# A layer's k/v projection by feature tiles over four odd token chunks, and its input's even halves made between the evacuations

## The chip, the cores and the metric

The kernel runs on one core of one Trainium2 chip. The core has five engines that work through queues of their own, each strictly in the order in which the program wrote its instructions: PE (TensorE, the matmuls), DVE (VectorE), ACT (ScalarE), POOL (GpSimd) and SP (SyncE, which here only issues DMAs). They wait for each other through semaphores. The metric is the device time of one execution in microseconds; the profile is one such execution, taken by the hardware profiler.

## The reference, cut to what matters

The reference is one inference step of a trunk of two layers over 1024 prompt tokens and 8 decode tokens, with a model width of 1024. Layer 1 is a retention layer, layer 2 a sliding-window attention layer with two k/v heads of 64 each. Each layer starts with an RMSNorm of its input and ends with an output projection that is added to its input.

```python
h = rmsnorm(x, g_norm)
proj = h @ w_in
q, k, v, gate = jnp.split(proj, [SWA_Q, SWA_Q + SWA_KV, SWA_Q + 2 * SWA_KV], axis=-1)
k = rmsnorm(k.reshape(B, L, SWA_KV_HEADS, SWA_HD), k_gain)
v = v.reshape(B, L, SWA_KV_HEADS, SWA_HD)
```

The change sits at the border of the two layers: at the end of layer 1's output projection, which makes x, and at the start of layer 2, which makes k and v (256 columns together) for all tokens before anything else.

## The kernel before, in words

**Numbers in two halves.** All float32 products are made of three matmuls on a rounded type: a number is split into a high part (ACT rounds it) and a low part (the number less its high part, on DVE or POOL), and high times high, high times low and low times high are added up in PSUM. Such a pair for a weight is called woh and wol in layer 1 and pw in layer 2; the pair for layer 2's input is A_hi and A_lo. It is kept in four pairs of tiles `AT[q]`, each for two tiles of 128 features and all tokens. `a_split(k, par)` makes the part of feature tile k for the even (par 0) or odd (par 1) chunks of 128 tokens, from a copy of x that `a_load` brings back from the scratch `xscr` in DRAM.

**Layer 1's output projection.** It is done in eight sets (`osets`): four groups of 256 features, in two parts that are summed. A set has seven products by a Strassen-like scheme, A11, A12, S4, S2, S1, S3 and A22, each for two halves t of the tokens; every (product, t) is a slot of 12 matmuls, so a set has 14 slots. The last set (group 3 in part 1) makes features 768 to 1023, which are feature tiles 6 and 7. S2 opens a new pair of banks `po`, S3 the next pair, and A22 adds on top of S3's banks once S3 has been read out of them. The read-outs (`o_evac`) are on ACT and DVE. Then `out_b` adds what part 0 left (`pa_add`), makes A_hi and A_lo of feature tiles 6 and 7 at once, stores x, and `out_sq` adds its squares to `acc`.

**The table.** In this stage the order of all engines but PE is written by a small planner, `Table`. `tb.slot` lists PE's slots with a clock of planned times, `tb.when(t, ...)` lists work that is written behind the slot in which time t lies, and `tb.later(n, ...)` work that is written behind slot n. `osets[7].n0` is the first slot of the last set and `e7` its planned time. Work listed behind slot n0 + 13 comes when all slots are written. `late` gives how many slots after a product `out_b` follows in the last set. The weights of the k/v projection are loaded by `kvs_load` and split by `kvs_conv`; those of the first q projection are loaded by `w0_load` into the same two raw tiles, so that SP's queue holds at these loads until a conversion has freed a tile.

**Layer 2's start.** Nine chunks of tokens (eight of the prompt, chunk 8 for the decode tokens) go through the projection in the order `KORD`: 1, 3, 5, 7, then 0, 2, 4, 6, 8. `kv_mm(c, h)` is half h of a chunk: four feature tiles of three matmuls into one bank. The loop over n writes half 0 of the next chunk, then half 1 of this one, and behind it the other steps of earlier chunks: `kv_ev` (norm of k through `knorm_a` and `knorm_b`: a square on ACT, kss on DVE, krk on POOL, kd on DVE; v on ACT and DVE), `kv_tr` (transposes of kd on PE into one of two banks `tr`) and `kv_kk` (keys out of that bank, on ACT and DVE). `rstd9` makes the norm factors r of layer 2's input from `acc`, once for the odd and once for the even chunks: small matmuls on PE, r and e on DVE, a power on POOL. `rb_dg`, `rb_mm` and `rb_ev` spread r over partitions: three scaled identity matrices (diagonals), a matmul with ones, and a copy to `rbc`. `a_dec` makes the decode columns of A, `xdec2` is the stationary tile of chunk 8's matmuls, copied from these columns. The conversions of the first weight sets (`wts[0].conv`, `wts[1].conv`) lie in the same loop, one piece per step, on ACT and POOL. Behind the loop starts `pair_proj`, the stream of q and gate projections, with q0; from there the matmuls are written by a credit scheme that the change does not touch.

Of the kernel before, what the change touches and what calls it, by code (L numbers as in the profile page):

```python
# [7 lines left out]
F32 = mybir.dt.float32  # L8
F32R = mybir.dt.float32r
AF = mybir.ActivationFunctionType  # L10
ALU = mybir.AluOpType
# [4 lines left out]
NP = 1024  # L16
ND = 8
NT = NP + ND
# [55 lines left out]
def _trunk(ctx, tc, nc, a):  # L74
# [588 lines left out]
    n = 0  # L663
# [610 lines left out]
    def a_dec():  # L1274
        nc.sync.dma_start(out=xscr[:, :, NP:NT].rearrange("f p n -> p f n"), in_=xd)
        xg = odT[:, 0:8, :]
        dve.tensor_tensor(xg, xd, gcol[:, 16:24].unsqueeze(2).broadcast_to([128, 8, ND]), MUL)
        for q in range(4):
            ahi, alo = [y[:, :, NP:NT] for y in AT[q]]
            dve.tensor_copy(ahi, xg[:, 2 * q:2 * q + 2, :])  # L1280
            dve.tensor_tensor(alo, xg[:, 2 * q:2 * q + 2, :], ahi.bitcast(F32), SUB)

    def o_slot(s, j, t):
# [16 lines left out]
        if done and t == 1:  # L1300
            late = {"A12": 6, "S1": 4, "S3": 2, "A22": 1}[name] if fin else {"S1": 5}.get(name, 2)
            tb.later(n + late, out_b if s.part else out_a, s, *done)
# [9 lines left out]
    for s in osets:  # L1312
# [28 lines left out]
        if s.part == 0:  # L1341
            tb.when(first["A22"] - 7.0, res_diff, s)
        elif s.q:
            tb.later(s.n0 + 11, pa_add, s, "p", pool)

# [124 lines left out]
    for i in range(4):  # L1470
        tb.when(e7 + 11.0 + 1.9 * i, kvs_conv, i)
    for j in range(2):
        tb.when(e7 + 13.5 + 3.5 * j, w0_load, j)
    for k in range(6):
        m = e7 + 3.1 + 2.0 * k
        tb.when(m - 5.0, a_load, k, 1)
        tb.when(m, a_split, k, 1)
    for k in range(2):
        tb.when(e7 + 11.0 + k, a_load, k, 0)
        tb.when(e7 + 15.6 + 2.0 * k, a_split, k, 0)  # L1480
    tb.ev.sort(key=lambda e: e[:2])
# [231 lines left out]

    def kv_mm(c, h):

        if h == 0:
            kvst[c] = (pjp.tile([128, 512], F32, tag="pj", name="pj") if KORD.index(c) % 4 < 2 else
                       scp.tile([128, 512], F32, tag="sc", name="sc"))
        ps = kvst[c]
        cs = slice(c * 128, c * 128 + 128)  # L1720
        for k in range(4 * h, 4 * h + 4):
            if c == 8:
# [55 lines left out]
    def rb_dg(ti):  # L1778
        t0, t1 = TG[ti]
        dg = io("sq", 2)  # L1780
        if ti == 2:
            nc.gpsimd.memset(dg[:, 256:264], 0.0)
        for i in range(3):
            c = t0 // 128 + i
            m = 128 if c < 8 else ND
            nc.vector.tensor_scalar(dg[:m, i * 128:i * 128 + m], ident[:m, :m], r9[:m, c:c + 1], None, ALU.mult)
        return dg
# [567 lines left out]

    dgs, rbs = {}, {}
    kv_mm(KORD[0], 0)
    for n in range(9):
        if n < 8:
            kv_mm(KORD[n + 1], 0)  # L2360
        if n == 1:
            rstd9(1)
        if n == 3:
            rstd9(0)
        if n >= 3:
            kv_tr(KORD[n - 3])
        kv_mm(KORD[n], 1)
        if n >= 4:
# [3 lines left out]
        if n >= 1:  # L2372
            kv_ev(KORD[n - 1])
        for k in ((), (2, 3), (4, 5))[n] if n < 3 else ():
            a_split(k, 0)
        if n == 2:
            a_dec()
# [6 lines left out]
        if 5 <= n <= 8:  # L2384
            wts[1].conv(n - 5)
        if n == 4:
            for q in range(4):
                nc.vector.tensor_copy(xdec2[:, 2 * q:2 * q + 2, 0:8], AT[q][0].bitcast(F32)[:, :, NP:NT])
                nc.vector.tensor_copy(xdec2[:, 2 * q:2 * q + 2, 32:40], AT[q][1].bitcast(F32)[:, :, NP:NT])
        for ti in list(dgs):  # L2390
# [14 lines left out]
    fill(ps, 1.5)  # L2405
    kv_kk(2)
    for ti in list(rbs):
        rb_ev(ti, rbs.pop(ti))
# [126 lines left out]
```

## Time and profile before

| | us |
|---|---|
| median of the three runs shown | 1329.73 (1326.33 to 1332.76) |
| the profiled execution | 1329.56 |
| its span, first to last instruction | 1327.7 |
| PE busy | 1275.8 (96% of the span) |
| DVE / ACT / POOL busy | 861.4 / 708.6 / 847.8 |
| last set of layer 1's output projection, first matmul | 860.5 |
| first matmul of the k/v projection | 886.5 |
| first matmul of q0 | 920.4 |

A row of the timeline has the start in us, the duration in us, the engine, the line, the operation with its output and input by their names, the shape and how many were merged; in brackets at the end stand the engine's idle time ahead of it and what ended that. Matmuls are pipelined, so the duration of one (0.28) is longer than the distance to the next (0.12). A row of a table of stages has the stretch, its length, the busy time of PE, weight loads, DVE, ACT and POOL with their counts, then the clock that TensorE was granted (1.00 is full speed), the DMA share and GB/s. A wait is put down to the one that came last by the profile.

### The profile page before, as it was taken

To read this page: it belongs to the slowest core of one execution; us is meant where nothing else is said; L and a number is where in the kernel's file an instruction comes from. 1 tells how busy PE (TensorE), PEld (TensorE's weight loads), DVE (VectorE), ACT (ScalarE), POOL (GpSimd) and SP (SyncE) were. 2 spreads that over 40 slices of the span, in tenths; PEclk is the share of its full clock that TensorE was granted. 3 is DMA by queue.
4 is the path that set the end of the run, shared out by engine and by line. 5 is a ranking of instruction groups with operands and counts; after the bars stand their busy time and mean duration, and the time that the engine had idled before them with its cause. 6 is when DMAs were issued, how large, how long until landed. Compare 5 with 4: busy or idle time off the path is not lost. (4 is left out here: it accounts for less than half of the span.)

```text
span 1327.7 us, 26879 instructions
## 1 busy us (share of the span) xinstructions
PE 1275.8 (96%) x9613; PEld 1231.6 (93%) x9613; DVE 861.4 (65%) x1682; ACT 708.6 (53%) x1746; POOL 847.8 (64%) x1006
## 2 busy tenths in 40 slices
PE   6999999999999999899999999988999999999998
PEld 6999999999999999788778998988999999998998
DVE  6953655665665664477788688786668777778411
ACT  5532545555556664466665254255666766666321
POOL 6643655656566664468899467765688787868410
PEclk9999999999999999999999999999999999999999
DMA  6313857586677763565776997562021120103532
GB/s 225 102 52 108 242 190 229 175 263 196 187 216 222 206 203 104 183 148 174 249 242 187 306 313 226 170 176 84 23 90 49 35 63 29 57 26 113 171 90 77
DMA packets 216155, 205.81 MB, mean 155 GB/s; under 512 B 19221, under 2 KB 185101, under 8 KB 216005
## 3 DMA queue, kind: packets, MB, share of 16 engines
q1 hardware_dynamic: 187696, 176.16, 43.6%
q10 hardware_dynamic: 28324, 27.94, 6.8%
q8 instruction: 76, 1.25, 0.4%
q14 instruction: 59, 0.48, 0.1%
HBM read 134.99 MB, written 70.09 MB: 154 GB/s over the span
## 5 line engine op out<-in xcount | busy, mean ns | idle before, releaser
L372 PE MATMUL b<-xh,woh 128*128 128x258 f32 x784 | 222.1, 283 | 0.0
L374 PE MATMUL b<-xh,wol 128*128 128x258 f32 x784 | 221.5, 283 | 0.0
L373 PE MATMUL b<-xl,woh 128*128 128x258 f32 x784 | 221.3, 282 | 0.0
L1632 PE MATMUL pj<-A_hi,pw 128*128 128x384 f32 (+1 forms) x512 | 173.1, 338 | 0.0
L1633 PE MATMUL pj<-A_lo,pw 128*128 128x384 f32 (+1 forms) x512 | 164.6, 321 | 1.0 <-POOL A_lo L1879 0.7
L1634 PE MATMUL pj<-A_hi,pw 128*128 128x384 f32 (+1 forms) x512 | 164.5, 321 | 0.0
L372 PEld LDWEIGHTS b<-xh,woh 128*128 128x128 f32 x784 | 148.1, 189 | 1.2
L373 PEld LDWEIGHTS b<-xl,woh 128*128 128x128 f32 x784 | 148.6, 190 | 0.0
L374 PEld LDWEIGHTS b<-xh,wol 128*128 128x128 f32 x784 | 148.0, 189 | 0.0
L366 PE MATMUL b<-wol,xh 128*128 128x256 f32 x448 | 126.7, 283 | 2.5 <-DVE wol L256 2.5
L365 PE MATMUL b<-woh,xh 128*128 128x256 f32 x448 | 126.5, 282 | 0.0
L367 PE MATMUL b<-woh,xl 128*128 128x256 f32 x448 | 126.3, 282 | 0.0
L314 POOL TENSOR_TENSOR yl<-yd,yh 128x256 fp32r<-128x256 f32 x64 | 57.0, 891 | 79.0 <-PE od L321 42.6
L256 DVE TENSOR_TENSOR wol<-s,woh 128x512 fp32r<-128x512 f32 x112 | 97.4, 876 | 10.1 <-ACT woh L251 9.5
L256 POOL TENSOR_TENSOR wol<-raw,woh 128x512 fp32r<-128x512 f32 x52 | 68.9, 1333 | 52.1 <-ACT woh L251 51.2
L1633 PEld LDWEIGHTS pj<-A_lo,pw 128*128 128x128 f32 x512 | 97.1, 190 | 1.6 <-POOL A_lo L1879 1.0
L1632 PEld LDWEIGHTS pj<-A_hi,pw 128*128 128x128 f32 x512 | 97.0, 189 | 0.6 <-issue 0.2
L1634 PEld LDWEIGHTS pj<-A_hi,pw 128*128 128x128 f32 x512 | 96.7, 189 | 0.0
L251 ACT ACTIVATE woh<-s 128x512 fp32r<-128x512 f32 x112 | 69.3, 623 | 43.6 <-POOL s L216 11.1
L2077 POOL TENSOR_TENSOR s<-s,sm 128x512 f32<-128x512 f32 x64 | 66.6, 1040 | 34.4 <-DVE sm L2076 33.7
L366 PEld LDWEIGHTS b<-wol,xh 128*128 128x128 f32 x448 | 85.2, 190 | 2.7 <-DVE wol L256 2.7
L251 ACT ACTIVATE woh<-raw 128x512 fp32r<-128x512 f32 x106 | 65.1, 624 | 42.1 <-PE po L1145 25.4
(431 smaller groups left out, 4134.5 us busy)
## 6 DMA issues: line engine op xcount, KB each, us to landing
raw<-in_w_in_ret_dram ACTq DMA_DIRECT2D x44, 512.0 KB
st<-in_state_ret_dram SPq DMA_DIRECT2D x64, 256.0 KB
out_dram<-st SPq DMA_DIRECT2D x64, 256.0 KB
vb<-vscr SPq DMA_DIRECT2D x64, 128.0 KB
evp<-qks SPq DMA_DIRECT2D x32, 256.0 KB
evw<-gsc SPq DMA_DIRECT2D x32, 256.0 KB
raw<-in_w_out_ret_dram SPq DMA_DIRECT2D x16, 512.0 KB
wr<-in_w_in_swa_dram SPq DMA_DIRECT2D x14, 512.0 KB
```

The costliest lines, as they stand in the source:

```text
L251: act(s.op[name, sub][0], src_of(s, name, sub), AF.Copy)
L256: eng.tensor_tensor(lo, src_of(s, name, sub), hi.bitcast(F32), SUB)
L365: mm(dst, xh, wh, start=a and i == 0, stop=False, skip_group_check=True)
L366: mm(dst, xh, wl, start=False, stop=False, skip_group_check=True)
L367: mm(dst, xl, wh, start=False, stop=z, skip_group_check=True)
L372: mm(dst, wh, xh, start=a, stop=False, **sg)
L373: mm(dst, wh, xl, start=False, stop=False, **sg)
L374: mm(dst, wl, xh, start=False, stop=z, **sg)
L1632: mm(ps, wh, AH(k)[:, t0:t1], start=first and k == ks[0], stop=False)
L1633: mm(ps, wh, AL(k)[:, t0:t1], start=False, stop=False)
L1634: mm(ps, wl, AH(k)[:, t0:t1], start=False, stop=last and k == ks[-1])
L2077: nc.gpsimd.tensor_tensor(u.st[:, :, 0:256], u.st[:, :, 0:256], u.sm.unsqueeze(2).broadcast_to([128, 2, 256]), ALU.mult)
```

## The change

In layer 1's last set, the splits of feature tiles 4 and 5 for the odd chunks and of tiles 0 and 1 for the even chunks are no longer written among the set's own evacuations but behind slots n0 + 14 and n0 + 17; the loads of the first two move to 16.0 and 16.5 on the planner's clock, those of the other two by one. A22's `out_b` comes one slot later, p's addition goes from slot 11 to slot 12, and the conversions of the k/v weights get new times.

In layer 2, `kv_mm` takes a range of feature tiles. PE does tiles 0 to 3 for the chunks 1, 3, 5 and 7, then tiles 4 and 5 for all four, with the norm factors of the odd chunks ahead of the last of these, and then 6 and 7 chunk by chunk in the loop. From chunk 0 on it goes by halves as before. The banks are dealt anew: the fifth chunk takes a bank of the pool `msp`. The splits of even tiles 2 to 5 come one step earlier in the loop. `a_dec` moves from step 2 to step 4 and writes the split of the decode columns straight into `xdec2`; the columns of A are copied from there after the loop (`a_decq`). The three diagonals of `rb_dg` move from DVE to ACT, and its zeroing from POOL to DVE.

```diff
@@ a_dec
-        for q in range(4):
-            ahi, alo = [y[:, :, NP:NT] for y in AT[q]]
-            dve.tensor_copy(ahi, xg[:, 2 * q:2 * q + 2, :])
-            dve.tensor_tensor(alo, xg[:, 2 * q:2 * q + 2, :], ahi.bitcast(F32), SUB)
+        dve.tensor_copy(xdec2[:, :, 0:8], xg)
+        dve.tensor_tensor(xdec2[:, :, 32:40], xg, xdec2[:, :, 0:8].bitcast(F32), SUB)
+
+    def a_decq(q):
+        for y, c0 in zip(AT[q], (0, 32)):
+            dve.tensor_copy(y[:, :, NP:NT], xdec2.bitcast(F32)[:, 2 * q:2 * q + 2, c0:c0 + 8])
@@ o_slot
-            late = {"A12": 6, "S1": 4, "S3": 2, "A22": 1}[name] if fin else {"S1": 5}.get(name, 2)
+            late = {"A12": 6, "S1": 4, "S3": 2, "A22": 2}[name] if fin else {"S1": 5}.get(name, 2)
...
-            tb.later(s.n0 + 11, pa_add, s, "p", pool)
+            tb.later(s.n0 + (12 if s.q == 3 else 11), pa_add, s, "p", pool)
...
     for i in range(4):
-        tb.when(e7 + 11.0 + 1.9 * i, kvs_conv, i)
+        tb.when(e7 + (9.0, 11.7, 14.6, 15.2)[i], kvs_conv, i)
...
     for k in range(6):
-        m = e7 + 3.1 + 2.0 * k
+        m = e7 + (3.1 + 2.0 * k if k < 4 else 19.0 + 0.5 * k)
         tb.when(m - 5.0, a_load, k, 1)
-        tb.when(m, a_split, k, 1)
+        if k < 4:
+            tb.when(m, a_split, k, 1)
+        else:
+            tb.later(osets[7].n0 + 14, a_split, k, 1)
     for k in range(2):
-        tb.when(e7 + 11.0 + k, a_load, k, 0)
-        tb.when(e7 + 15.6 + 2.0 * k, a_split, k, 0)
+        tb.when(e7 + 12.0 + k, a_load, k, 0)
+        tb.later(osets[7].n0 + 17, a_split, k, 0)
@@ kv_mm
-    def kv_mm(c, h):
-
-        if h == 0:
-            kvst[c] = (pjp.tile([128, 512], F32, tag="pj", name="pj") if KORD.index(c) % 4 < 2 else
+    def kv_mm(c, ks):
+
+        if ks[0] == 0:
+            kvst[c] = (pjp.tile([128, 512], F32, tag="pj", name="pj") if KORD.index(c) in (0, 1, 5, 6) else
+                       msp.tile([128, 512], F32, tag="ms", name="pm") if KORD.index(c) == 4 else
                        scp.tile([128, 512], F32, tag="sc", name="sc"))
...
-        for k in range(4 * h, 4 * h + 4):
+        for k in ks:
@@ rb_dg
-            nc.gpsimd.memset(dg[:, 256:264], 0.0)
+            nc.vector.memset(dg[:, 256:264], 0.0)
...
-            nc.vector.tensor_scalar(dg[:m, i * 128:i * 128 + m], ident[:m, :m], r9[:m, c:c + 1], None, ALU.mult)
+            act(dg[:m, i * 128:i * 128 + m], ident[:m, :m], AF.Copy, scale=r9[:m, c:c + 1])
@@ the loop over the chunks
-    kv_mm(KORD[0], 0)
+    for k in (0, 4):
+        for c in KORD[:4]:
+            kv_mm(c, range(k, (4, 6)[k // 4]))
+            if (k, c) == (4, 5):
+                rstd9(1)
     for n in range(9):
-        if n < 8:
-            kv_mm(KORD[n + 1], 0)
-        if n == 1:
-            rstd9(1)
+        if 3 <= n < 8:
+            kv_mm(KORD[n + 1], range(4))
...
-        kv_mm(KORD[n], 1)
+        kv_mm(KORD[n], range(6 if n < 4 else 4, 8))
...
-        for k in ((), (2, 3), (4, 5))[n] if n < 3 else ():
+        for k in ((2, 3), (4, 5), ())[n] if n < 3 else ():
             a_split(k, 0)
-        if n == 2:
+        if n == 4:
             a_dec()
...
-        if n == 4:
-            for q in range(4):
-                nc.vector.tensor_copy(xdec2[:, 2 * q:2 * q + 2, 0:8], AT[q][0].bitcast(F32)[:, :, NP:NT])
-                nc.vector.tensor_copy(xdec2[:, 2 * q:2 * q + 2, 32:40], AT[q][1].bitcast(F32)[:, :, NP:NT])
...
     kv_kk(2)
+    for q in range(4):
+        a_decq(q)
```

## The prediction

> **What bounds the kernel now.** I read the page first, for the engine that is busy nearly all the time, then the table of stages around the change, then the timelines of PE, DVE, ACT and POOL from 860 to 925 us.
>
> ```profile
> span 1327.7 us, 26879 instructions
> PE 1275.8 (96%) x9613; PEld 1231.6 (93%) x9613; DVE 861.4 (65%) x1682; ACT 708.6 (53%) x1746; POOL 847.8 (64%) x1006
> ```
>
> ```profile
> 860.50:877.80 17.30, 17.30 (x146) 17.26 (x144) 16.60 (x18) 13.24 (x24) 14.27 (x13) 1.00 0.80 222
> 877.80:886.50 8.70, 4.60 (x26) 4.46 (x25) 7.91 (x12) 1.06 (x2) 6.12 (x6) 0.80 0.18 37
> ...
> 900.00:920.40 20.40, 16.86 (x131) 15.36 (x129) 14.90 (x59) 10.30 (x41) 12.04 (x14) 1.00 0.32 85
> 920.40:990.00 69.60, 69.60 (x489) 68.59 (x487) 47.39 (x121) 45.56 (x131) 49.82 (x67) 1.00 0.20 62
> ```
>
> Columns: stretch, its length, then busy PE, weight load, DVE, ACT, POOL, granted clock, DMA share, GB/s. PE bounds the kernel except between 877.8 and 920.4, which is where the change works. It idles twice there: 4.1 us before the last product of layer 1 (A22), and 3.5 us in pieces in the k/v projection. After 920.4 PE is full for 70 us, so what is won before that moves everything behind it.
>
> ```profile
> 874.95 0.28 PE L1144 MATMUL po<-oxh,woh 128*128 128x258 f32 x1
> 877.70 0.28 PE L1146 MATMUL po<-oxh,wol 128*128 128x258 f32 x1
> 882.07 0.36 PE L1144 MATMUL po<-oxh,woh 128*128 128x258 f32 x1 [4.10 <-DVE evw L1179]
> 886.53 0.28 PE L1726 MATMUL pj<-pw,A_hi 128*128 128x256 f32 x1
> 903.84 0.41 PE L104 MATMUL tr<-ident,kd 128*128 128x128 f32 x2 [0.78 <-DVE r L1657]
> 906.70 0.36 PE L1726 MATMUL sc<-pw,A_hi 128*128 128x256 f32 x1 [1.03 <-DVE kd L1707]
> 914.04 0.88 PE L1792 MATMUL o<-sq,ones 128*128 128x384 f32 x2 [0.98 <-DVE sq L1786]
> 920.06 0.68 PE L1792 MATMUL o<-sq,ones 128*128 128x264 f32 x2 [0.76 <-ACT pw L1616]
> 920.39 0.53 PE L1632 MATMUL pj<-A_hi,pw 128*128 128x384 f32 x1
> ```
>
> The bracket gives the idle time and its releaser. A22 adds into the bank that S3 left, so it must wait until DVE has read S3 out (L1179). The 24 matmuls of S3 took 2.9 us (874.95 to 877.8); the 24 of A22 took 4.46 (882.07 to 886.53). The clock explains that:
>
> ```profile
> 73.78 0.58 PE L366 MATMUL b<-wol,xh 128*128 128x256 f32 x1 [2.51 <-DVE wol L256]
> 813.96 0.39 PE L1146 MATMUL po<-oxh,wol 128*128 128x258 f32 x1 [1.48 <-DVE wol L256]
> 73.80:77.00 3.20, 3.20 (x15) 3.20 (x16) 2.94 (x5) 0.98 (x2) 0.53 (x2) 0.50 0.03 5
> 814.00:817.00 3.00, 3.00 (x23) 2.84 (x24) 2.90 (x7) 0.15 (x1) 2.68 (x2) 1.00 0.03 9
> 883.00:886.10 3.10, 3.10 (x16) 3.10 (x16) 2.31 (x2) 0.72 (x1) 2.48 (x3) 0.50 0.23 21
> ```
>
> After idles of 4.10 and 2.51 us the granted clock was 0.50 for over 3 us; after 1.48 it stayed 1.00. The Trainium skill ("TensorE: Matmul & The Clock Gate", section "Why this matters for your kernels") warns only of idle gaps above about 3 us; the row at 73.78 shows 2.51 to be enough here. By the page an idle of 2 us would be safe; by these rows it is open between 1.48 and 2.51.
>
> **The change, part by part.** *1. Splits 4 and 5 (odd) and 0 and 1 (even) leave the last set.*
>
> ```profile
> 869.41 1.69 DVE L1272 SCALAR_TENSOR_TENSOR A_lo<-ar,gcol,A_hi 128x512 fp32r<-128x512 f32 x1
> 869.23 1.31 POOL L216 TENSOR_TENSOR s<-raw 128x512 f32<-128x512 f32 x1 [1.24 <-PE S L1145]
> 871.01 0.68 DVE L256 TENSOR_TENSOR wol<-s,woh 128x512 fp32r<-128x512 f32 x1
> 873.99 1.78 DVE L1272 SCALAR_TENSOR_TENSOR A_lo<-ar,gcol,A_hi 128x512 fp32r<-128x512 f32 x1
> 877.90 1.42 DVE L1272 SCALAR_TENSOR_TENSOR A_lo<-ar,gcol,A_hi 128x512 fp32r<-128x512 f32 x1
> 880.52 0.73 DVE L1272 SCALAR_TENSOR_TENSOR A_lo<-ar,gcol,A_hi 128x512 fp32r<-128x512 f32 x1
> 881.51 0.74 DVE L1179 TENSOR_TENSOR evw<-po,evw 128x258 f32<-128x258 f32 x2
> ```
>
> DVE has 16.60 busy of 17.30 us in this set, so it is what is late. A large DVE subtraction takes 0.68 alone and 1.4 to 1.8 when POOL is already inside one: POOL's s runs 869.23 to 870.54, and DVE's A_lo of 869.41 ends 0.56 after it. Three splits go from ahead of the S3 read-out (rows 873.99, 877.90, 880.52: 3.9 us recorded), the fourth from behind it. Not all of it returns, because step 2 puts POOL work under what is left. Replaying the new order with a DVE operation that waits for the POOL operation in front of it (POOL about 1.2, DVE then 0.57): wol of S1 ends 872.9 instead of 871.7, the odd split 3 at 873.5, wol of S3 at 875.25, the split of c at 876.25, wol of A22 at 878.0, and after four read-outs (a pair takes 0.74) S3 is out at 879.4. A22 starts at 879.45, 2.6 us earlier. The bounds: all large operations at 0.68 give a start at PE's own end, 878.0; all at 1.7 give 880.9. I take the replay, as it follows rows pair by pair.
>
> New wait: PE's first wl matmul of S1 stands at 872.3 before (874.95 less the 2.88 of a product, and two matmuls on) and would wait 0.6 for wol; S3 then ends at 878.45, so the idle before A22 is 1.0. That is below 1.48: the clock stays full and A22 takes 2.9, saving 1.6. The projection starts at 882.3 instead of 886.53: 4.2 us.
>
> *2. Weight conversions.* Conversion 0 moves a slot ahead. ACT waits in it for S4's matmuls to free the tiles, so split 3 and the weights behind it on ACT slip some 2 us, which ACT's slack covers (13.24 of 17.30 busy); DVE's split 3 would pay first. On POOL, conversions 2 and 3 now run back to back, and the addition of p goes behind them instead of between. Its result is wanted only by A22's read-out, so this costs nothing there; w's addition behind it ends at about 884.0, where ACT and DVE are still busy with x.
>
> *3. The loads.*
>
> ```profile
> 875.25 9.23 SPq L1421 DMA_DIRECT2D raw<-in_w_in_swa_dram  x2
> ```
>
> The loads of splits 4 and 5 are moved past the first of these two weight loads on SP's queue, which waits for conversion 1 on POOL, and stay ahead of the second, which held the queue until 884.5 before. Issued about 876, wanted at 884.7: covered by 8 us.
>
> *4. Feature tiles over four chunks.* Four chunks times four features times three matmuls is 48, at 0.12 each (row pitch of the 24 in 2.88) 5.7 us; features 4 and 5 are needed at 888.0. The moved splits follow A22's read-out on DVE (886.2) and end at 886.85 and 887.5: covered, with 1.1 us left, then PE would wait for them. Behind them on DVE and ACT stand the squares; the sums for the odd chunks end on POOL about 890.1, just when PE comes to them (890.1). PE ends them at about 891.1. Then come r, 2.4 later (1.0 of it on POOL), and the chunks' own chain:
>
> ```profile
> 893.64 1.03 POOL L120 TENSOR_TENSOR r<-r,mhalf 128x4 f32<-128x4 f32 x1 [1.11 <-DVE e L1658]
> 894.64 0.70 POOL L120 TENSOR_TENSOR krk<-kss,mhalf 128x2 f32<-128x2 f32 x1
> 895.90 1.41 DVE L1272 SCALAR_TENSOR_TENSOR A_lo<-ar,gcol,A_hi 128x512 fp32r<-128x512 f32 x2
> 899.82 2.12 DVE L1272 SCALAR_TENSOR_TENSOR A_lo<-ar,gcol,A_hi 128x512 fp32r<-128x512 f32 x2
> 901.86 0.21 DVE L1277 TENSOR_TENSOR odT<-xd,gcol 128x64 f32<-128x64 f32 x1
> 903.20 0.17 DVE L1281 TENSOR_TENSOR A_lo<-odT,A_hi 128x16 fp32r<-128x16 f32 x1
> 908.05 0.61 DVE L1707 SCALAR_TENSOR_TENSOR kd<-sc,krk,kgb 128x128 f32<-128x128 f32 x2 [0.62 <-POOL krk L120]
> 908.58 0.17 DVE L2388 CAST xdec<-A_hi 128x16 fp32r<-128x16 f32 x1
> ```
>
> Chunk 1's norm moves only from 894.6 to about 894.2, since its matmuls now end at 892.5. But the splits of 895.90 now precede it, in the wait for r (1.4), and the nine decode operations of 901.86 to 903.37 (1.5) become three behind chunk 7. With 0.7 less of waiting for POOL in the pairs, chunk 7's kd ends at 904.65 instead of 908.66: 4.0.
>
> *5. Decode tile and diagonals.* The eight xdec copies (0.08 apart, 0.7) go; eight copies back into A come behind chunk 2's keys, under q0's matmuls (DVE 47.39 of 69.60 busy there). Uncovered they would cost 0.7. Each group of three diagonals moves from DVE (1.2 us) to ACT:
>
> ```profile
> 908.75 0.37 ACT L1741 ACTIVATE vo<-sc,r 128x128 f32<-128x128 f32 x1 [6.06 <-DVE kd L1707]
> 909.02 0.62 ACT L1616 ACTIVATE pw<-raw 128x512 fp32r<-128x512 f32 x1
> 910.62 0.63 ACT L1616 ACTIVATE pw<-wr 128x512 fp32r<-128x512 f32 x1
> 914.96 0.49 ACT L1797 ACTIVATE rbc<-o 128x384 f32<-128x384 f32 x1 [1.84 <-PE o L1792]
> ```
>
> ACT becomes the engine that orders the last four chunks. From vo on: vo 0.27 (908.75 to 909.02), three rounds of 1.60 (909.02 to 910.62), nine diagonals at vo's 0.27 (2.4), two rbc at 0.39, one more conversion and kkh (0.8): 9.0. With the last product, q0 starts 9.5 after kd instead of 11.7 (908.66 to 920.39): 2.2. A diagonal has no row of its own; 0.27 and vo's whole 0.37 bound it, 0.9 in all. The Trainium skill ("ScalarE: Activation LUTs", section "Rules for kernel authors") budgets about 0.3 us plus 0.83 ns per element, an estimate of 0.41 for 128; by that the end would be 1.3 later and the kernel at 1324.7. The vo row at 0.27 to the next disagrees.
>
> *6. Banks.* The fifth chunk uses the bank ms, read out by then; the 1.03 of 906.70 should go.
>
> **Sum.** q0 starts at 914.2 instead of 920.39. Of the 6.2, 4.2 is the earlier start and 2.0 the phase: 33.9 before, 31.9 after, against 30.3 of PE work (33.9 less 3.55 of idle). The profiled execution took 1329.56, its span 1327.7 and 1.86 around it; the median shown is 0.17 above. 1329.56 - 6.2 = 1323.4.
>
> **Rivals.**
> *PE sets the pace.* If the side engines keep up, q0 starts after 2.9 and 30.3 us of work from 878.0: 911.2, a gain of 9.2, 1320.4. For it: ACT has slack on average. Against: one order per engine, and norms that go ACT, DVE, POOL, DVE.
> *The clock falls anyway.* If POOL's locks hold S3's read-out to 880.9, the idle is 2.5 and A22 runs at half clock: 1.2 won at the start instead of 4.2, 1326.4. For it the gap between 1.48 and 2.51 in the rows; against it the replay.
> *It does little.* r waits for the last squares and not for PE; if the moved splits push them 4 us, kd stays: only 2.2 of the tail is left, 1327.4.
> *Slower:* PE stops in order at the odd sums of squares. POOL adds w's only after DVE has added x's, and both now stand behind two more splits. Ready at 890.1 in my replay, with no slack; every microsecond later costs one, and past 2.5 the clock falls (1.6 more). It decides from 4.6 late on, as 4.6 + 1.6 is all that was won; at 7 late: 1331.9. Four operations at 1.8 for 0.7 would do it; against it, POOL is idle there, waiting for these very sums.
>
> **How the numbers follow.** Chances: the sum with its bounds (gain 4.5 to 7.5) 0.54, PE's pace 0.16, clock and little together 0.17, slower 0.13. 0.5%, about what a measurement of this kernel can tell from no change, is 6.65 us: the first case is over it with half of its weight, the second wholly; faster 0.43. The third and the rest of the first give same 0.44, the fourth 0.13. The range runs from PE's pace, 1320, to the clock and part of the little case, 1328.
>
> **What would show it.** The idle before A22 at about 1 us and clock 1.00 through it; kv_mm from about 882; no wait at features 4 and 5; an idle under 1 us at the sums; ACT without gaps from vo to the last rbc; q0 near 914, and then the same distance to the end. A 0.50 after A22's start, a PE wait on A_lo or acc, or a late xscr load would make me wrong.

## The result, and the profile after

| | before | after |
|---|---|---|
| median of 19 runs each, side by side | 1329.36 us (1325.08 to 1334.82) | 1324.46 us (1319.25 to 1327.8) |
| profiled execution | 1329.56 | 1325.47 |

The ratio is 0.9957, with a 95% interval of 0.9942 to 0.9971: 3.9 to 7.7 us faster. The forecast was 1323.4, 6.2 us faster.

The executions of the kernel before spread over 9.7 us and those of the kernel after over 8.6, so the pair of traces is compared by a length inside them: from the first matmul of layer 1's last set to the first matmul of q0. I call it the stage. It is read from PE's timeline, and it repeats: two executions of the kernel after gave 55.25 and 55.30. All lines that the change touches work in it, apart from the copies back into A just behind. The pair of profiled executions differs by 4.4 in span: 1.54 less ahead of the stage, 4.60 less in it, and 1.75 more behind it. Apart from those copies the code ahead of the stage and behind it is the same in both, and there one kernel differs as much from itself: behind the stage, two executions of the kernel after took 409.05 and 406.85, and the kernel before 407.31. So only the 4.60 is put down to the change; the last section says what moves the rest.

The span and the busy times from the page of the kernel after, and its table of stages in the columns of the prediction (stretch, length, busy PE, weight load, DVE, ACT, POOL, clock, DMA share, GB/s):

```profile
span 1323.3 us, 26867 instructions
PE 1275.1 (96%) x9613; PEld 1230.1 (93%) x9613; DVE 859.0 (65%) x1668; ACT 710.5 (54%) x1755; POOL 849.5 (64%) x1005
```

```profile
860.50:877.80 17.30, 16.20 (x133) 15.79 (x132) 16.64 (x19) 11.07 (x20) 14.88 (x13) 1.00 0.74 205
877.80:886.50 8.70, 7.71 (x65) 7.74 (x66) 7.63 (x14) 5.56 (x10) 4.33 (x6) 1.00 0.79 201
900.00:920.40 20.40, 19.11 (x135) 17.61 (x134) 11.99 (x46) 13.62 (x52) 13.72 (x16) 1.00 0.41 112
```

In the second stretch, where PE had worked 4.60 of 8.70 us at a clock of 0.80, it works 7.71 at 1.00 (the stretches lie at the same times as those of the prediction; the stage itself starts 1.54 earlier). PE's timeline of the kernel after (the first row is the start of the stage, the last its end):

```profile
859.00 0.28 PE L1144 MATMUL S<-oxh,woh 128*128 128x258 f32 x1
871.32 0.39 PE L1146 MATMUL S<-oxh,wol 128*128 128x258 f32 x1 [0.39 <-DVE wol L256]
878.79 0.36 PE L1144 MATMUL po<-oxh,woh 128*128 128x258 f32 x1 [1.71 <-DVE evw L1179]
881.76 0.28 PE L1732 MATMUL pj<-pw,A_hi 128*128 128x256 f32 x1
889.56 0.95 PE L1656 MATMUL tr<-onec,acc 128*128 128x1 f32 x8
899.15 0.41 PE L104 MATMUL tr<-ident,kd 128*128 128x128 f32 x2 [0.88 <-DVE r L1662]
914.25 0.54 PE L1637 MATMUL pj<-A_hi,pw 128*128 128x384 f32 x1
```

The wait ahead of A22 is 1.71 instead of 4.10; A22 takes 2.97 (878.79 to 881.76) instead of 4.46. A new wait of 0.39 stands at the set's first S1 matmul with wol.

The stage in pieces, worked out from such rows for every run of the study, in us. "A22 starts" is counted from the stage's start; "vo" is the first read-out of v for chunk 7 (ACT, behind that chunk's kd); the last three columns are lengths.

| run | A22 starts | idle ahead of it | A22 takes | projection's start to vo | vo to q0 | stage |
|---|---|---|---|---|---|---|
| before | 21.53 | 4.10 | 4.46 | 22.22 | 11.63 | 59.85 |
| after | 19.79 | 1.71 | 2.97 | 22.31 | 10.17 | 55.25 |
| last set's edits alone | 19.78 | 1.70 | 2.98 | 23.16 | 11.33 | 57.25 |
| feature tiles alone | 21.52 | 4.07 | 4.47 | 23.91 | 11.62 | 61.52 |
| decode and diagonals alone | 21.50 | 4.06 | 5.30 | 20.79 | 10.17 | 57.76 |
| after, split 4 back in the set | 20.33 | 2.24 | 4.47 | 22.31 | 10.19 | 57.29 |
| after, c's squares later | 18.16 | 0.07 | 2.98 | 24.15 | 10.19 | 55.48 |
| after, zeroing on POOL | 19.79 | 1.69 | 2.96 | 22.38 | 10.85 | 55.99 |
| after, diagonals on DVE | 19.80 | 1.72 | 2.96 | 22.38 | 11.32 | 56.45 |
| after without feature tiles | 19.79 | 1.70 | 2.97 | 21.72 | 10.18 | 54.66 |
| the same, new banks, no zeroing | 19.80 | 1.72 | 2.97 | 21.74 | 9.63 | 54.14 |
| the same, c's squares later | 18.18 | 0.09 | 2.96 | 23.74 | 9.63 | 54.50 |
| after, once more | 19.79 | 1.72 | 2.96 | 22.38 | 10.18 | 55.30 |

So of the 4.60 that the change won in the stage, 3.23 is the earlier start of the projection (1.74 by A22's start and 1.49 by its length), 1.46 the tail from vo to q0, and the middle, from the projection's start to vo, is 0.09 longer.

### The profile page after: what moved, and what is told of

The parts are those of the page before. It is cut to its first block, busy times and chain, and to the rows that moved or that the text cites. A ratio compares the mean times of both kernels' runs of the same rounds, so it can differ in the third digit from the quotient of the medians.

```text
span 1323.3 us, 26867 instructions
## 1 busy us (share of the span) xinstructions
PE 1275.1 (96%) x9613; PEld 1230.1 (93%) x9613; DVE 859.0 (65%) x1668; ACT 710.5 (54%) x1755; POOL 849.5 (64%) x1005
```

## The experiments

The theory was that of the prediction: three parts, each with a gain of its own. The first question is whether that holds part by part.

**The last set's edits alone.** The kernel before, with the planner's edits only (splits 4 and 5, even splits 0 and 1, their loads, the conversion times, p's addition and A22's `out_b`):

```diff
-            late = {"A12": 6, "S1": 4, "S3": 2, "A22": 1}[name] if fin else {"S1": 5}.get(name, 2)
+            late = {"A12": 6, "S1": 4, "S3": 2, "A22": 2}[name] if fin else {"S1": 5}.get(name, 2)
...
-        m = e7 + 3.1 + 2.0 * k
+        m = e7 + (3.1 + 2.0 * k if k < 4 else 19.0 + 0.5 * k)
...
+            tb.later(osets[7].n0 + 14, a_split, k, 1)
```

> The kernel before with the edits of the last set alone (splits, loads, conversions, p's addition, A22's out_b); the k/v projection keeps its halves, the decode tile and the diagonals stay. The stage is counted from the last set's first matmul to q0's first: 59.85 us before, 55.25 after the whole change. My theory: DVE is relieved here and nowhere else, so the idle before A22 is 1.7 us instead of 4.1, the clock stays 1.00 and the projection starts 22.8 after the set's start instead of 26.0; by halves it wants feature tiles 4 and 5 about 3 us after its start, when they are just ready (0 to 0.5 of a wait), and the sums of squares 0.7 to 1.5 before they are; the stage takes 56.5 to 58. Rival: without the order by feature tiles PE waits for the moved splits for 2 us and more, and the stage takes 59 or more.

1324.98 against 1327.57, ratio 0.9985 (0.9971 to 0.9999). The stage is 2.60 shorter than before; the start of the projection is 3.23 earlier, exactly as in the whole change, and part of that is lost again behind it (23.16 to vo instead of 22.22). PE's timeline of this run:

```profile
878.55 0.36 PE L1144 MATMUL po<-oxh,woh 128*128 128x258 f32 x1 [1.70 <-DVE evw L1179]
887.99 1.05 PE L1654 MATMUL tr<-onec,acc 128*128 128x1 f32 x8 [0.51 <-POOL acc L1249]
```

With the order of before, PE comes to the sums of the odd chunks early and waits 0.51 for POOL's last sum: up to there the side engines set the pace, not PE. Chunk 1's kd starts 32.53 us after the stage's start instead of 34.83, so 2.30 of the 3.23 get through.

**Feature tiles alone.** The kernel before, with `kv_mm` over ranges of features, the new banks, the new place of the odd norm factors, and the even splits 2 to 5 one step earlier:

```diff
-    kv_mm(KORD[0], 0)
+    for k in (0, 4):
+        for c in KORD[:4]:
+            kv_mm(c, range(k, (4, 6)[k // 4]))
+            if (k, c) == (4, 5):
+                rstd9(1)
...
-        for k in ((), (2, 3), (4, 5))[n] if n < 3 else ():
+        for k in ((2, 3), (4, 5), ())[n] if n < 3 else ():
```

> The kernel before with the new order of the projection alone (feature tiles over four chunks, the new banks, the splits of even tiles 2 to 5 one step earlier). My theory: idle of 4.1 and half clock before and in A22 stay, the projection starts 26.0 after the set's start; its length goes from 33.9 to 32.5 to 33.5, as the splits leave the norm chain but the decode operations stay in it; stage 58.5 to 59.5. Rival, the order by tiles is what the gain comes from: length 31 to 32, stage 57 to 58.

1331.24 against 1327.57, ratio 1.0024 (1.0006 to 1.0042), and a stage 1.67 longer. By itself this part costs time, and both theories on record, which had it gain, were missed. The loss is there at chunk 1, whose kd starts at 38.02 from the stage's start instead of 34.83; the run without the tiles, below, shows how it comes about. Later PE waits for r of the even chunks, and the clock falls (timeline, then table of stages):

```profile
901.38 0.41 PE L104 MATMUL tr<-ident,kd 128*128 128x128 f32 x2 [2.50 <-DVE r L1657]
```

```profile
901.30:905.00 3.70, 3.62 (x22) 3.65 (x23) 2.00 (x8) 0.00 (x0) 3.53 (x5) 0.68 0.32 108
```

**Decode tile and diagonals alone.** The kernel before, with `a_dec` writing into `xdec2` at step 4, the copies back behind the loop, the diagonals on ACT and the zeroing on DVE:

```diff
-            nc.gpsimd.memset(dg[:, 256:264], 0.0)
+            nc.vector.memset(dg[:, 256:264], 0.0)
...
-            nc.vector.tensor_scalar(dg[:m, i * 128:i * 128 + m], ident[:m, :m], r9[:m, c:c + 1], None, ALU.mult)
+            act(dg[:m, i * 128:i * 128 + m], ident[:m, :m], AF.Copy, scale=r9[:m, c:c + 1])
```

> The kernel before with the decode tile and the diagonals alone (decode split straight into xdec2 behind chunk 7, columns of A copied after the loop, diagonals on ACT). My theory: the nine decode operations leave the norm chain (1.4), and the last four chunks go 0.3 to 0.5 faster each; the projection takes 31 to 32.5 instead of 33.9, stage 57 to 58.5. Rival: the chain is bound by POOL's powers anyway and ACT takes over in the last chunks; length 33 to 34, stage 59 to 60.

1324.72 against 1327.57, ratio 0.9981 (0.9963 to 0.9999). Projection start to vo is 1.43 shorter and vo to q0 1.46 shorter, 2.9 together. The stage won 2.09, since A22 was 0.84 longer than in the kernel before after the same idle:

```profile
879.61 0.55 PE L1144 MATMUL po<-oxh,woh 128*128 128x258 f32 x1 [4.06 <-DVE evw L1179]
```

```profile
879.60:883.00 3.40, 3.39 (x16) 3.40 (x17) 2.61 (x4) 0.72 (x1) 2.78 (x4) 0.50 0.09 14
883.00:884.90 1.90, 1.90 (x10) 1.90 (x10) 1.66 (x2) 0.72 (x1) 1.20 (x2) 0.50 0.91 276
```

The slow stretch lasted through all 5.3 us of A22 here. With an A22 of the old length, this part would have won 2.9.

The two parts that win, 2.60 and 2.09, make 4.69 together; the whole change won 4.60. Is the third part then worth nothing, or does it pay only once the start is earlier? That was asked next.

**The change without the feature tiles.** The kernel after, with `kv_mm` by halves, its banks and the steps of the even splits as before:

```diff
-    for k in (0, 4):
-        for c in KORD[:4]:
-            kv_mm(c, range(k, (4, 6)[k // 4]))
-            if (k, c) == (4, 5):
-                rstd9(1)
+    kv_mm(KORD[0], 0)
...
-        for k in ((2, 3), (4, 5), ())[n] if n < 3 else ():
+        for k in ((), (2, 3), (4, 5))[n] if n < 3 else ():
```

> The changed kernel without its order by feature tiles: the edits of the last set, the decode tile and the diagonals, with the projection by halves, its banks and its even splits as before. Alone, the last set's edits gave a stage of 57.25 us, the decode tile and diagonals 57.76, the tiles 61.52 (before 59.85, whole change 55.25). My theory: the first two add up and the tiles only cost, so the projection starts at 22.8, takes 31 to 32 and the stage is 53.8 to 54.8, shorter than in the changed kernel. Rival: once the last set's splits are late, the tiles are what gives them time; without them PE waits 1 us and more for features 4, 5 and the sums, and the stage is 55.3 or longer.

1321.38 against 1327.94, ratio 0.9955 (0.9940 to 0.9970). Its stage is 54.66, 5.19 shorter than before and 0.59 shorter than with the tiles. So the change that gives this document its title costs 0.59 within the change and 1.67 by itself. The run takes back two things at once, the order of the matmuls and the earlier place of the even splits. Where the time goes is seen in the timelines. First DVE of the kernel after, from r of the odd chunks on (L1662), with the first pair of moved splits (L1272), the steps of chunk 1's norm (kss, kd), and chunk 7's kd as the last row:

```profile
890.54 0.17 DVE L1662 TENSOR_SCALAR r<-tr 128x4 f32<-128x4 f32 x1 [1.05 <-PE tr L1656]
890.82 1.41 DVE L1272 SCALAR_TENSOR_TENSOR A_lo<-ar,gcol,A_hi 128x512 fp32r<-128x512 f32 x2
892.76 0.23 DVE L1705 TENSOR_SCALAR kss<-kss,e 128x2 f32<-128x2 f32 x1 [0.53 <-ACT kj L1704]
893.81 0.61 DVE L1712 SCALAR_TENSOR_TENSOR kd<-pj,krk,kgb 128x128 f32<-128x128 f32 x2 [0.42 <-POOL krk L120]
903.37 0.61 DVE L1712 SCALAR_TENSOR_TENSOR kd<-sc,krk,kgb 128x128 f32<-128x128 f32 x2 [0.62 <-POOL krk L120]
```

POOL of the kernel after (the last addition of squares, the power for r, chunk 1's krk):

```profile
885.91 2.28 POOL L1249 TENSOR_TENSOR acc<-acc,sq 128x516 f32<-128x516 f32 x1 [3.69 <-ACT sq L1248]
891.00 1.46 POOL L120 TENSOR_TENSOR r<-r,mhalf 128x4 f32<-128x4 f32 x1 [1.61 <-DVE e L1663]
893.08 0.70 POOL L120 TENSOR_TENSOR krk<-kss,mhalf 128x2 f32<-128x2 f32 x1 [0.62 <-DVE kss L1705]
```

PE and ACT of the kernel after (the first matmul of chunk 1's features 6 and 7, behind the sums of 889.56, and chunk 1's square kj, which needs the last of them):

```profile
891.16 0.28 PE L1732 MATMUL pj<-pw,A_hi 128*128 128x256 f32 x1
892.07 0.22 ACT L1704 ACTIVATE kj<-pj 128x64 f32<-128x64 f32 x1 [2.97 <-PE pj L1734]
```

And the run without the tiles, on PE, DVE and POOL:

```profile
889.88 0.83 PE L1656 MATMUL tr<-onec,acc 128*128 128x1 f32 x6 [0.49 <-POOL acc L1249]
```

```profile
891.03 0.15 DVE L1662 TENSOR_SCALAR r<-tr 128x4 f32<-128x4 f32 x1
893.19 0.61 DVE L1712 SCALAR_TENSOR_TENSOR kd<-pj,krk,kgb 128x128 f32<-128x128 f32 x2
904.43 0.61 DVE L1712 SCALAR_TENSOR_TENSOR kd<-sc,krk,kgb 128x128 f32<-128x128 f32 x2 [0.62 <-POOL krk L120]
```

```profile
891.46 1.02 POOL L120 TENSOR_TENSOR r<-r,mhalf 128x4 f32<-128x4 f32 x1 [0.46 <-DVE e L1663]
892.46 0.70 POOL L120 TENSOR_TENSOR krk<-kss,mhalf 128x2 f32<-128x2 f32 x1
```

Counted from the stage's start (860.54, 859.00, 860.65), the starts of these steps:

| | before | after | without the tiles |
|---|---|---|---|
| r of the odd chunks on DVE | 32.66 | 31.54 | 30.38 |
| krk of chunk 1 on POOL | 34.10 | 34.08 | 31.81 |
| kd of chunk 1 on DVE | 34.83 | 34.81 | 32.54 |
| kd of chunk 7 on DVE | 47.51 | 44.37 | 43.78 |

With the tiles, the last sum is there at 888.19 (885.91 and 2.28), but PE comes to it only at 889.56, and DVE stands idle for 1.05 until PE has been there: r is 1.16 later than without them. Chunk 1's norm then waits for PE once more. Its last two features stand behind the sums, so ACT can start on kj only at 892.07; kss on DVE waits for kj (0.53), and krk on POOL for kss (0.62). Without the tiles kj had run at 888.58, ahead of r, and krk follows the power for r at once. So krk comes 2.54 behind r instead of 1.43, and chunk 1 is 2.27 later.

The moved splits lie in this wait and don't lengthen it: they end on DVE at 892.23, and POOL's power, which takes 1.46 beside them instead of 1.02, ends at 892.46, ahead of kss. From chunk 1 to chunk 7 the kernel after saves 1.68, as no splits are left between chunks 3 and 5; 0.59 stays lost. By these rows the order of the matmuls costs 2.27 and the earlier place of the splits gives 1.68 of it back; no run has the one without the other. The whole start of 3.2 us that the last set's edits had won was used up at chunk 1 (34.81 against 34.83).

**Split 4 back in the last set.** This asks what a split in the set costs, and whether the clock bears the longer idle:

```diff
-        m = e7 + (3.1 + 2.0 * k if k < 4 else 19.0 + 0.5 * k)
+        m = e7 + (3.1 + 2.0 * k if k < 5 else 19.0 + 0.5 * k)
...
-        if k < 4:
+        if k < 5:
             tb.when(m, a_split, k, 1)
```

> The changed kernel with the odd split of feature tile 4 put back among the last set's evacuations, ahead of the S3 read-out on DVE. It lengthens the idle before A22 from 1.7 us to 2.4 to 3.3. By the rows of before (half clock after 2.51, full after 1.48) the granted clock falls to 0.50 for A22, its 24 matmuls take 4.4 instead of 3.0, and the projection starts 2.2 to 3.1 later than in the changed kernel. Rival, by the page's about 3 us (the Trainium skill, TensorE: Matmul & The Clock Gate, section Why this matters for your kernels): the clock stays 1.00 and the projection starts 0.7 to 1.6 later.

One execution, 1322.77. The stage is 57.29 instead of 55.25:

```profile
878.73 0.36 PE L1144 MATMUL po<-oxh,woh 128*128 128x258 f32 x1 [2.24 <-DVE evw L1179]
```

```profile
878.70:883.00 4.30, 4.27 (x23) 4.30 (x24) 3.27 (x5) 2.15 (x4) 2.75 (x4) 0.60 0.82 233
```

A22 starts 0.54 later, and behind an idle of 2.24 the clock falls: 4.47 for A22 instead of 2.97. So 1.50 of the 2.04 that this split costs in this execution is the clock. The last section shows that an idle of this length does not always end so.

**The squares of c later.** In the prediction's replay A22 would start 2.6 earlier; it started 1.74 earlier. DVE and POOL of the kernel after:

```profile
873.89 1.59 DVE L1237 SCALAR_TENSOR_TENSOR A_lo<-evc,gcol,A_hi 128x512 fp32r<-128x512 f32 x1
875.74 1.44 DVE L256 TENSOR_TENSOR wol<-raw,woh 128x512 fp32r<-128x512 f32 x1
```

```profile
873.64 1.29 POOL L1249 TENSOR_TENSOR acc<-acc,sq 128x516 f32<-128x516 f32 x1
```

The split of c (L1237) runs beside POOL's addition of squares, which began 0.25 ahead of it and ended at 874.93. The test moves the addition behind the read-outs:

```diff
-        tb.later(tb.n + (1 if s.q == 3 else 2), out_sq, s, key, par)
+        tb.later(tb.n + (3 if (s.q, key) == (3, "c") else 1 if s.q == 3 else 2), out_sq, s, key, par)
```

> The changed kernel with the squares of c written two slots later, so that POOL's sum of them no longer stands in front of DVE's split of c. My theory: that split takes 1.59 us because POOL's sum starts 0.25 us ahead of it; with the sum behind, it takes 0.7, the S3 read-out comes 0.8 earlier and the idle before A22 is 0.8 to 1.0 instead of 1.71; stage 54.3 to 54.6. Rival: POOL then starts its conversion in the same place and DVE waits for that instead; idle 1.5 to 1.8, stage 55.1 to 55.4.

One execution, 1322.65. DVE and PE:

```profile
874.93 0.74 DVE L1237 SCALAR_TENSOR_TENSOR A_lo<-evc,gcol,A_hi 128x512 fp32r<-128x512 f32 x1
875.93 0.68 DVE L256 TENSOR_TENSOR wol<-raw,woh 128x512 fp32r<-128x512 f32 x1
```

```profile
885.75 0.39 PE L1732 MATMUL sc<-pw,A_hi 128*128 128x256 f32 x1 [1.56 <-DVE evp L1181]
```

The split takes 0.74 instead of 1.59, wol 0.68 instead of 1.44, and the idle ahead of A22 is 0.07. So the addition of squares is what held the split of c. The run gives back 1.63, more than the missing 0.9, as wol is faster too. But the stage is 55.48, no shorter, and the expectation was missed: PE, 1.62 earlier at the projection, waits 1.56 for the bank of its third chunk, which A22's read-out frees. That read-out came later than in the kernel after (25.23 from the stage's start instead of 24.09), and the test itself made it late. The moved addition ran on POOL from 880.69 to 882.43, ahead of w's addition; ACT waited 3.53 for that one, DVE's split of w waited for ACT, and the read-out stands behind this split.

**Zeroing on POOL, and diagonals on DVE.** Two runs that take the tail apart, both from the kernel after. The first gives the zeroing of `dg` back to POOL, the second gives it back and puts the diagonals on DVE again:

```diff
-            nc.vector.memset(dg[:, 256:264], 0.0)
+            nc.gpsimd.memset(dg[:, 256:264], 0.0)
```

```diff
-            act(dg[:m, i * 128:i * 128 + m], ident[:m, :m], AF.Copy, scale=r9[:m, c:c + 1])
+            nc.vector.tensor_scalar(dg[:m, i * 128:i * 128 + m], ident[:m, :m], r9[:m, c:c + 1], None, ALU.mult)
```

> The changed kernel with the zeroing of eight columns of the last diagonal tile back on POOL. My theory: on DVE it stands behind kd of the seventh chunk and holds ACT for 0.45 us ahead of the last diagonal, and with ACT the last rbc copies and PE's last product; on POOL it comes earlier, the 1.04 of idle before that product falls to 0.5 to 0.7, stage 54.7 to 54.9. Rival: POOL's own queue (conversion and power) is as late; stage 55.2 to 55.4.

> The changed kernel with the nine diagonals back on DVE and the zeroing on POOL. My theory: the last four chunks are again ordered by DVE and POOL at 3.0 us a chunk instead of about 2.7 on ACT, and the time from vo to q0 goes from 10.2 to 11.2 to 11.7 (it was 11.6 before); stage 56.2 to 56.8. Rival: the move only shifted the load; vo to q0 stays 10 to 10.5, stage 55.0 to 55.5.

One execution each, 1322.87 and 1321.23. ACT of the kernel after, of the run with POOL's zeroing, and PE of the run with the diagonals on DVE:

```profile
904.08 0.37 ACT L1747 ACTIVATE vo<-sc,r 128x128 f32<-128x128 f32 x1 [5.45 <-DVE kd L1712]
906.45 0.98 ACT L1792 ACTIVATE sq<-ident,r 128x128 f32<-128x128 f32 x3
907.33 0.37 ACT L1762 ACTIVATE kkh<-tr 128x256 fp32r<-128x256 f32 x1
912.91 0.30 ACT L1792 ACTIVATE sq<-ident,r 8x8 f32<-8x8 f32 x1 [0.45 <-DVE sq L1788]
```

```profile
911.34 0.30 ACT L1792 ACTIVATE sq<-ident,r 8x8 f32<-8x8 f32 x1 [1.07 <-POOL sq L1788]
```

```profile
907.79 0.88 PE L1798 MATMUL o<-sq,ones 128*128 128x384 f32 x2 [1.44 <-DVE sq L1792]
```

With the diagonals on DVE, vo to q0 is 11.32, 1.15 longer. Three diagonals on ACT hold it for 0.88 (906.45 to 907.33). The zeroing is a new wait that the change brought: the last group's diagonal waits 0.45 for DVE's memset, which stands behind chunk 4's kd. On POOL it is worse, against the expectation: 1.07, and a tail of 10.85. With the diagonals on DVE, POOL's zeroing held nothing up.

**No zeroing, new banks, no feature tiles.** From the run without the tiles: the banks of the change, and the zeroing replaced by a factor of 1 in the unused rows, so that one ACT operation writes all 128 rows of the decode diagonal:

```diff
-        if ti == 2:
-            nc.vector.memset(dg[:, 256:264], 0.0)
...
-            act(dg[:m, i * 128:i * 128 + m], ident[:m, :m], AF.Copy, scale=r9[:m, c:c + 1])
+            act(dg[:, i * 128:i * 128 + m], ident[:, :m], AF.Copy, scale=r9[:, c:c + 1])
...
+    nc.vector.memset(r9, 1.0)
```

> The kernel without the order by feature tiles (stage 54.66 us), with the new banks for the last five chunks and with the zeroing dropped: the last diagonal is written over all 128 partitions from the identity, so its zeros come with it and ACT waits for no other engine there. My theory: the 0.61 of idle at the seventh chunk's bank goes with the banks, and the last 0.50 before PE's last product shrinks; stage 53.4 to 54.3, which is 1 to 1.9 shorter than in the changed kernel, and the time 1 to 2 us below it. Rival: both waits stand beside the norm chain, which sets q0 anyway; stage 54.4 to 54.8.

1320.80 against 1327.23, ratio 0.9946 (0.9918 to 0.9973). Its stage is 54.14, the shortest of all, with a tail of 9.63 instead of 10.17. The wait of 0.45 for the memset is gone from ACT, and a wait of 0.61 for a bank is gone from PE. The way to vo, behind that bank, stays as it was, so the 0.54 of the tail is put down to the zeroing; the two were not run apart.

**The same with c's squares later.** Here the addition is moved by four slots, behind w's `out_b`, to see whether the missing 0.9 of the start is worth something when the tiles are gone:

```diff
+        tb.later(tb.n + (4 if (s.q, key) == (3, "c") else 1 if s.q == 3 else 2), out_sq, s, key, par)
```

> The kernel of the run before this one with the squares of c moved behind out_b of w, into a stretch where POOL waits. My theory: A22 starts 18.2 us after the set's start, as in the run with the squares two slots later, but now w's addition is not held up, so the sums for the odd chunks come no later than before; q0 is set by the chain from these sums, and the stage gains 0.3 to 0.8: 52.8 to 53.8. Rival: PE's earlier start is lost at the bank of the third chunk, which waits for A22's read-out, and the sums come when they came; stage within 0.2 of the run before.

1322.05, ratio 0.9956 (0.9940 to 0.9973). The projection starts 1.64 earlier, and the stage is 54.50, 0.36 longer. PE's timeline:

```profile
883.85 0.39 PE L1735 MATMUL pj<-pw,A_lo 128*128 128x256 f32 x1 [0.84 <-DVE A_lo L1273]
```

PE comes to feature tile 4 before its split and waits there. The reason is on DVE (the split of w, then the pair of splits of tiles 4 and 5):

```profile
881.35 0.75 DVE L1238 SCALAR_TENSOR_TENSOR A_lo<-evw,gcol,A_hi 128x512 fp32r<-128x512 f32 x1 [2.10 <-ACT A_hi L1237]
882.69 1.77 DVE L1273 SCALAR_TENSOR_TENSOR A_lo<-ar,gcol,A_hi 128x512 fp32r<-128x512 f32 x2
```

DVE waits 2.10 for ACT's half of w, and ACT had waited 2.29 for w's addition on POOL, which comes no earlier than before. So A22's read-out, behind the split of w, starts at 24.00 from the stage's start instead of 24.08, although A22 is 1.62 earlier. From the splits of tiles 4 and 5 on, DVE works without a gap up to r in both runs, for 6.08 here and for 5.62 in the run before; the pair of splits took 1.41 there, without the moved addition of squares beside it (on POOL from 881.92 to 883.24). r of the odd chunks starts 0.37 later, and the stage is longer by as much. The expected gain of 0.3 to 0.8 was missed. So in these rows an earlier A22 brings r no earlier, as its read-out hangs on w's addition. What the idle that is left ahead of A22, 1.7 us, is worth when w's addition comes earlier too was not tried.

**The kernel after, once more,** beside the last two on the same chip:

> The changed kernel once more, beside the two above. The stage should repeat within 0.2 of 55.25, whatever the clock does elsewhere; the time against the kernel before 0.994 to 0.998.

1321.73, ratio 0.9963 (0.9950 to 0.9975), stage 55.30. By the stage, the kernel without the tiles and the zeroing beats it by 1.16 us, and the kernel before by 5.71. By the time of whole executions, 0.9946 (0.9918 to 0.9973) against 0.9963 (0.9950 to 0.9975), the two aren't told apart.

## Why the prediction was right, and where it was not

The time lies 1.1 us from the forecast of 1323.4 and in its range. By the prediction's bound of 0.5% the change, 0.43%, is the case "same", to which it gave 0.44 against 0.43 for "faster"; the interval of the ratio holds both. That the times agree so well is in part luck: the change won 4.60 in the stage, not 6.2, and the spread of single executions covers the difference. In the stage the forecast of 6.2 was 4.2 of start and 2.2 of tail, less 0.2 that it had the middle grow by (22.4 from 882.3 to kd, against 22.2); measured were 3.23, 1.46 and a middle 0.09 longer. Two terms were too large, and the order in the title was never set against the old one.

*1. The last set: right, mis-sized.* The read-out of S3 does come earlier, the idle shrinks and the clock holds, A22 runs in 2.97, and the new wait at S1 is there (0.39 for 0.6). But A22 starts 1.74 earlier, not 2.6, and the idle is 1.71, not 1.0. The replay let the split of c go first and take 0.66; POOL's addition of squares was 0.25 us ahead, and the split took 1.59. With that addition moved it took 0.74. So 4.2 became 3.23.

*2 and 3. Conversions and loads: right.* In the kernel after PE waits for neither in the stage. The largest waits on the moved loads are ACT's, 0.47 and 0.15 at 887.5 and 888.4.

*4. Feature tiles: the chain right, the credit wrong.* Counted from the stage's start, the forecast had the sums and PE meet at 29.56 (890.1 less 860.54). The sums were ready at 29.19 and PE came at 30.56, 1.0 late, as the projection had started 1.0 later than forecast and the new order puts 66 matmuls ahead of the sums (four chunks by four features, three chunks by two, three each) where the old one had 48. That chunk 1's norm follows the end of its own matmuls, and that the moved splits fit into the wait, was forecast and came so; but the norm was to gain 0.4 (894.6 to 894.2), and krk gained 0.02. Chunk 7's kd was forecast 4.0 earlier and came 3.14 earlier: 0.4 of the difference lies at chunk 1, the rest behind it. What failed is the credit. The prediction booked this under the order by feature tiles, but what wins there are the start, the decode step and the place of the splits; the order itself keeps the start from reaching chunk 1. The prediction set the whole phase against the kernel before and never the tile order against the old order with the new start. That comparison gives a loss of 0.59.

*5. Decode tile and diagonals: right, a bit too large.* Alone they win 1.43 ahead of vo (forecast 1.5 for the decode operations) and 1.46 behind it. The forecast for the tail was 9.5 from the end of chunk 7's kd, and it took 10.27 (10.17 from vo). Of the difference, 0.45 is the wait for the moved zeroing, which the prediction named in no step; the run without tiles and zeroing has 9.63 from vo. A diagonal takes 0.29 (0.88 for three) against the 0.27 forecast. The Trainium skill ("ScalarE: Activation LUTs", section "Rules for kernel authors") would give an estimate of 0.41 for it; the row stands nearer to vo's 0.27, so here the forecast by rows was the better one.

*6. Banks: a small thing either way.* The 1.03 at 906.70 is gone, but it was not the fifth chunk's: it is the seventh chunk that waits there, for the bank that kd of the third has to free, and the seventh now takes another. Without the tiles and with the old banks 0.61 of it is left (`sc` behind kd, at 903.08); the new banks take that away too, but the way to vo stays as it was (21.74 against 21.72).

*The rivals.* PE did not set the pace of the whole phase: it still idles 2.16 us in the projection, though at chunk 1 all wait for it. The clock did not fall; in the run with split 4 back, 0.53 us more of idle came with a fall and cost 2.04 in all. The rival in which the moved splits push the last squares, so that the change does little, did not come true: the sums were ready 2.2 earlier than in the kernel before (29.19 from the stage's start instead of 31.40). The slower rival, POOL late at the odd sums, was wrong by its sign: POOL was 1.4 us ahead of PE.

## What to carry to other kernels

When a change has several parts, set each part against the kernel with the others in place, not against the old one: here the part in the title lost time, and the two others made the gain. An order of matmuls that keeps PE busy is worth nothing where the chain of small operations (sums, r, norms) sets the end; there PE should have the first chunk done, and come to the sums, as early as the sums are ready. And when an operation is moved to another engine, follow also the small operations that it has to wait for: a memset of eight columns cost 0.45.

## What the runs showed of the hardware

*The clock.* Ahead of A22, idles of PE of 1.69 to 1.72 us were followed by full clock in all seven traces that have them, idles of 4.06 to 4.10 by a half clock in all three, and the one of 2.24 by a half clock. But the length of the idle alone doesn't decide. The kernel before idled 2.51 us near its start and lost its clock (the row at 73.78 of the prediction); the run without the feature tiles idled as long ahead of the same matmul and kept it (timeline, then table of stages):

```profile
73.86 0.39 PE L366 MATMUL b<-wol,xh 128*128 128x256 f32 x1 [2.47 <-DVE wol L256]
73.90:77.00 3.10, 3.10 (x26) 3.10 (x27) 2.91 (x5) 1.09 (x3) 0.52 (x1) 1.00 0.02 5
```

Nor is a shorter idle always safe: in the run with POOL's zeroing, 1.30 us at 1254.71 with nine small transposes behind it came before a half clock. What else decides, no run here shows. The Trainium skill ("TensorE: Matmul & The Clock Gate", section "Why this matters for your kernels") names gaps above about 3 us; here 2.24 and 2.51 were enough in some executions. The slow stretches have one length here, wherever they begin: in windows of 0.1 us the granted clock is 0.50 for 3.4 us (73.8 to 77.2 and 882.8 to 886.1 in the kernel before, 879.1 to 882.4 with split 4 back), or for twice that (878.2 to 884.9 with the decode tile and diagonals alone, where it began while PE still idled). So A22, 2.97 at full clock, takes 4.46 or 5.30.

The same thing moves the time of whole executions where the code is alike. In the profiled execution after, PE idled 1.19 us near its start, where the one before had idled 2.51 and lost its clock. Near its end it was the other way round: here the clock fell behind an idle of 2.12, and in the execution before PE had idled 1.08 there, at 1.00. Timeline and table of stages of the kernel after:

```profile
72.66 0.39 PE L366 MATMUL b<-wol,xh 128*128 128x256 f32 x1 [1.19 <-DVE wol L256]
1257.16 0.68 PE L104 MATMUL tr<-ident,rbc 16*128 16x16 f32 x9 [2.12 <-DVE rbc L2208]
```

```profile
1257.00:1260.00 3.00, 2.84 (x16) 2.81 (x17) 0.29 (x2) 0.28 (x1) 0.00 (x0) 0.61 0.21 67
```

In both traces the clock falls once more some microseconds later, so the kernel after has one slow stretch more at its end and one less at its start. This is part of the 1.54 and 1.75 outside the stage, and a reason to measure an effect of a few us by the length of its own stage.

*DVE and POOL.* A DVE subtraction of 128x512 took 0.74 by itself and 1.59 beside a POOL addition that had begun 0.25 us earlier; it ended 0.55 after it. The other way round, POOL's power for r took 1.46 when a DVE split had begun 0.18 earlier, and 1.02 without it. In these rows the one that starts first keeps its pace. The Trainium skill ("SBUF — State Buffer", section "Who interferes with whom") says that issue order decides who blocks, and these rows agree; what the prediction's replay got wrong was the order, by a quarter of a microsecond.
